# Issuing each pass of a float32r product as two matmuls of 256 columns

## The chip, the cores and the metric

The kernel runs on one core of one Trainium2 chip. The metric is the device time of that core in microseconds. The profile gives the time from the first to the last instruction (the span) of one execution, and the clock granted to TensorE in each stretch (1.00 is 2.4 GHz, 0.5 is 1.2 GHz).

## The reference, cut to what matters

Four residual layers act on 512 tokens of 1024 features, all in float32. Layers 0 and 1 have a mixer and a feed-forward part, each with a modulated norm; blocks 2 and 3 have mixers of several gated branches and a feed-forward part with a short convolution. Nearly all arithmetic is in products of activations with weights, such as

```
def swiglu(h, w_gate, w_up, w_down):
    return (jax.nn.silu(h @ w_gate) * (h @ w_up)) @ w_down

def mixer_ssd_mla(h, positions, w_in, ...):
    z, xbc, dt_raw, q_a, kv_a, k_pe = split_cols(h @ w_in, L0_SIZES)
    ...
    return jnp.concatenate([y_ssd, o_mla], axis=-1) @ w_out
```

with 512 rows in h, 1024 to 5000 columns in the input weights of the mixers and 2816 hidden features in each feed-forward part (two products up, one down). Between them stand state space scans, gated linear attention, causal and sparse attention, convolutions and norms.

## The kernel before, in words

Activations lie by feature: a tile has 128 features on the partitions and the 512 tokens along the free axis. A float32 product is made of three passes of float32r parts. A weight block [128, 128] is split into a high and a low part (whi by ScalarE, L364; wlo by VectorE, L365), and so is each activation tile (tiles named h for the input of a layer, s for others). The function mm3 (L246) issues the three passes whi·xhi, whi·xlo, wlo·xhi into one PSUM bank of 128 x 512 float32; the weights are the stationary operand and the tokens the moving one. In the trace every matmul has its own LDWEIGHTS, under the engine PEld.

The callers of mm3 are these:

- gemm_group (L269): two m-tiles of output in the banks named pg, all k-tiles of one after all of the other, 512 tokens at a time. The weights come from wtiles (L222) in sets of at most 8 blocks, [128, 1024], so a set serves 24 passes.
- gemm_wide (L302): 3 or 4 m-tiles side by side (banks pg and pa) at the start of a product whose input becomes ready tile after tile. Where the input comes by halves of the tokens, the matmuls have 256 columns already.
- gemm_tail (L281): the last m-tiles of a product by halves of the tokens, also in matmuls of 256 columns, with the norm's work (L387, L421, L2264, L2296) between them.

gemm_tok (L334) has the same three passes with the operands exchanged (L349 to L351): the activations are stationary and the weights move, 512 columns in two of its products and 256 in two others. One of the latter (the values of block 2) takes, for two groups of heads out of three, every fourth token as the stationary operand.

The instructions of each engine are put in order beforehand by a scheduler, by the priority that each had when it was traced (`cur_priority`, which counts instructions); an instruction whose operands are not ready yields to the next. Helpers such as `paced` and `later` shift these priorities, so that the products of a layer run between the small instructions of its attention and scans (L824 to L844, L1940 to L1952 and others). The first matmul into a bank has `start=True`, which clears the whole bank.

Of the kernel before, what the change touches and what calls it, by code (L numbers as in the profile page):

```python
# [26 lines left out]
# order of the work: priorities and steps between what runs side by side, slots and tiles of the phases  # L27
# [21 lines left out]
class Core:  # L49
    """Helpers shared by the layers: weight streaming, float32 products in three passes of float32r  # L50
    parts, norms over features. Activations by feature live in slots of 4 KB a partition."""
# [27 lines left out]
    def consts(self, group, t=None, queue=None):  # L79
        """Load a group of constants, not before the instruction of self.mark has been issued."""  # L80
        if t is None:
            t = self.s4([128, self.a[group].shape[1]])
        if self.mark is None:
            (queue or self.nc.scalar).dma_start(t, self.a[group])
        else:
            with self.tc.issue_after(self.mark.ins):
                self.nc.scalar.dma_start(t, self.a[group])
        self.groups[group] = t
# [12 lines left out]
    # ---- memory: tiles of one tag are handed out in the order traced, so streams of work that are to  # L101
    # run side by side have tags of their own
    @contextmanager
    def psum(self, **banks):
        """The banks of the streams a and b, for the phases in the block."""
        with self.tc.tile_pool(name=self.nm("ps"), bufs=1, space=PSUM) as self.xpool:
            self.banks = banks
            yield
# [28 lines left out]
    def s4(self, shape=(128, 2, T), dt=F32, tag="s4"):  # L137
        """A slot of 4 KB a partition of the phase."""
        return self.spool.tile(list(shape), dt, tag=tag, name=self.nm(tag), bufs=self.nslots[tag] if isinstance(self.nslots, dict) else self.nslots)

    def fa(self, dt=F32, tag="s4"):
        """Tiles of features [128, T], two to a slot, taken when first used."""
# [11 lines left out]
    def h4(self, i, dt=F32):  # L154
        """Slot i % 8 (two tiles of features) of the memory of the input of a layer, free for float32, or for
        float32r parts, in place of those before."""
# [6 lines left out]
    def ha(self, slots, dt=F32):  # L163
        """As fa, in slots of the input of a layer."""
# [11 lines left out]
    def parts(self, tag="s4"):  # L176
        """Tiles of features as float32r parts: x(k) = (high, low). Tag h: the input of a layer."""
# [8 lines left out]
    @contextmanager  # L186
    def later(self, by):
        """What the block traces yields to what is traced up to `by` instructions after it."""
        at = self.tc.cur_priority
        self.tc.cur_priority = at + by  # L190
        yield
        self.tc.cur_priority = at

    @contextmanager
    def paced(self, by):
        """Products traced in the block, and what belongs to them, run between what is traced after it: a step
        of 3 passes every `by` instructions."""
# [10 lines left out]
    def beside(self):  # L208
        """What the block traces has the priority of what is traced after it."""
# [4 lines left out]
    def step(self, at):  # L214
        """The priority of one step of paced products, counted from at."""
# [6 lines left out]
    def wtiles(self, src, blocks):  # L222
        """At most 8 blocks [128, 128] of weights, as float32r parts [128, 1024]."""
# [12 lines left out]
    def wload(self, w, m0, nm, k0, nk):  # L236
        """m-tiles m0.. and k-tiles k0.. of a packed weight [m, 128, k, 128], as float32r parts: nm times a
        function of k."""
# [7 lines left out]
    def mm3(self, ps, w, x, first, last):  # L246
        (wh, wl), (xh, xl) = w, x
        mm = lambda *a, **k: self.nc.tensor.matmul(*a, **k, skip_group_check=True)  # L248
        i = mm(ps, wh, xh, start=first, stop=False)
        mm(ps, wh, xl, start=False, stop=False)  # L250
        self.mm_mark = mm(ps, wl, xh, start=False, stop=last)
        return i

    def gemm(self, w, x, evac, m0=0, nm=None, wide=False, tail=0):
        """For each m-tile of packed w: evac(m, PSUM [128, T]) of w^T x; x(k) gives float32r parts, to be
        scaled by token after the product if there is x.rows. Wide: 4 m-tiles at first, for tiles of x that
        become ready one after the other, or 3 by halves of the tokens where x does. Tail: the last m-tiles
        by halves of the tokens, with evac(m, PSUM of the half, its slice)."""
# [22 lines left out]
    def gemm_tail(self, w, x, evac, m0, n):  # L281
        """At most 24 blocks of weights, loaded once. What follows the first half runs under the second."""
# [19 lines left out]
    def gemm_wide(self, w, x, evac, m0, n):  # L302
# [5 lines left out]
        for half in halves:  # L308
            for k in range(nk):
# [3 lines left out]
                for m in range(n):  # L313
                    # the first product of a bank clears it for both halves
# [19 lines left out]
    def gemm_tok(self, w, x, evac, n0=0, n=None):  # L334
        """By token: evac(j, PSUM [128, n]) of x^T w for the 4 tiles of tokens; w packed [128, k, N], n <= 512."""
# [5 lines left out]
        for k0 in range(0, nk, kc):  # L341
            kk = min(kc, nk - k0)
            hi, lo = (t.rearrange("p (k n) -> p k n", n=n) for t in self.wtiles(w[:, k0 : k0 + kk, n0 : n0 + n], kk * n // 128))
            for q in range(kk):
                k = k0 + q
                wh, wl = hi[:, q], lo[:, q]
                for j in range(4):
                    xh, xl = x(k, j)
                    nc.tensor.matmul(pss[j][:, :n], xh, wh, start=k == 0, stop=False)  # L349
                    nc.tensor.matmul(pss[j][:, :n], xl, wh, start=False, stop=False)  # L350
                    nc.tensor.matmul(pss[j][:, :n], xh, wl, start=False, stop=k == nk - 1)  # L351
# [8 lines left out]
    def split(self, hi, lo, src, scale=None):  # L360
        """hi + lo = src (times a per-partition scale), both float32r."""
# [10 lines left out]
    def sq_acc(self, acc, src, first, scale=1.0):  # L372
        """acc (+)= (src scale) squared."""
# [8 lines left out]
    def tok_sums(self, tiles, p=None, first=True, last=True):  # L382
        """[128, 4] by token in PSUM: sums over the partitions of all tiles. Not first: added to a bank with sums."""
# [6 lines left out]
    def pow_rstd(self, p, n, eps, pool=False):  # L390
        """(p / n + eps) ** -0.5 for a few columns p."""
# [8 lines left out]
        # Newton's method, from half the exponent: 3.5e-2, 2e-3, 5e-6, rounding  # L400
# [7 lines left out]
    def rstd_tok(self, tiles, n, eps=EPS, pool=False):  # L408
        """[128, 4] by token: (sum over partitions and tiles / n + eps) ** -0.5."""
        return self.pow_rstd(self.tok_sums(tiles), n, eps, pool)  # L410

    def bcast_tok(self, r):
        """[128, 4] by token -> PSUM [128, T], the same on every partition."""
# [4 lines left out]
    def bcast_to(self, p, r, j0):  # L418
        """[128, n] by token, of the tiles j0.. of tokens, into p."""
# [19 lines left out]
    def norm_h(self, r, x, gain, shift=None, update=None, h=None, half=slice(0, T)):  # L439
        """float32r parts of x rows gain (+ shift), by feature; r [128, T] the rows. update(k) completes x(k).  # L440
        With h: the half of the tokens of h."""
# [20 lines left out]
    def set_rows(self, h):  # L462
        """At the start of a phase: the factors by token that its input lacks, on all partitions."""
# [5 lines left out]
    def ffn(self, h, up, down, conv, end):  # L469
        """down^T (silu(gate) * val), with gate and val through a causal convolution of 3 where conv gives  # L470
        its taps; end() gives the evac of the product and what follows it."""
# [29 lines left out]
def _cols(w, idx):  # L501
    """Columns of w by index, zeros where it is -1, packed as [m, 128, k, 128]."""
# [13 lines left out]
def _tok(w):  # L516
    """[K, N] as [128, K / 128, N]."""
# [3 lines left out]
def _pv(a):  # L521
    """A vector by feature as [128, n]."""
# [9 lines left out]
def _taps(w):  # L532
    """[taps, channels] -> [128, channels / 128 * taps]."""
# [8 lines left out]
# l0_w_in: z 0, xbc 1024, dt 2560, q_a 2576, kv_a 2960, k_pe 3216  # L542
# [5 lines left out]
# l1_w_in: gq 0, gk 512, gv 1024, glr 2048, gg 2064, nq 3088, kc vc ks vs kw vw 3600 + 128 i, ngate 4368  # L548
# [26 lines left out]
# w_in_2: q 0, k 768, v 1536, conf_a 2304, conf_gate 3072, sc_b 3840, sc_c 4608, sc_x 5376, gates 6144 + 1024 b  # L575
# [23 lines left out]
# w_in_3: r k v 512 i, wl 1536, al 1600, gl 1664, qkv 1792, z 3328, a 3840, b 3844, gate_a 3848, gate_b 4872  # L599
# [90 lines left out]
def _lvl(s, u):  # L690
    """For each level of halves of 2 ** l tokens: s in the first and t in the second half of one block."""
# [6 lines left out]
def _lvls(f, n, levels, odd):  # L698
    """For each level f(p, 128 level + u), at the columns u < n in the first (odd: second) halves of blocks."""
# [29 lines left out]
def _dist2(p, u, dil, span):  # L729
    """p + span - u steps back, of dil tokens each; 1e30 outside 0 .. 128 steps."""  # L730
# [40 lines left out]
class Layer0:  # L771
    """SSD and latent attention, with the input and output projections."""
# [21 lines left out]
    def conv_evac(self, out, ps, w, taps, bias=None):  # L794
        """out[t] = bias + sum_s w(taps - 1 - s) ps[t - s]: a causal convolution along the free axis."""
# [8 lines left out]
    def silu_half(self, out, u):  # L804
        """out = silu(2 u)."""
# [5 lines left out]
    def softplus(self, out, x, shape):  # L811
        """out = max(x, 0) + ln(1 + exp(-|x|))."""
# [7 lines left out]
    def attn_scores(self, q, k, w, bias, l, m=None):  # L820
        """exp(s - max s) of s = q^T k + bias for one block of 128 queries, and its sums l."""
# [9 lines left out]
    def attn_pv(self, o, p, w, v, even=True):  # L831
        """o [128 queries, dv] += p v, with v(kb) the values of key block kb."""
# [13 lines left out]
    def pipeline(self, units, steps=1):  # L846
        """Run generators with each step of a unit traced next to the step before of the unit after it. Steps: those
        after the first of the last unit."""
# [124 lines left out]
    def attn_out(self, out, ot, blk):  # L973
        """[128 tokens, 512 features] into 4 tiles by feature."""
# [8 lines left out]
    def l0_ssd(self, xbc, zs, misc, cs, fill):  # L983
        """silu(z) (y + d x) of the state space scan into the tiles of x, by chunks of 128 tokens and 4 heads
        at a time."""
        nc = self.nc
        # steps, decays
# [96 lines left out]
class Layer1:  # L1084
    """Gated linear attention and native sparse attention. The selection holds every block of keys
    (there are no more blocks than it selects) and the window every key, so both are causal attention
    over all keys, whatever the compressed scores."""
# [1444 lines left out]
```

## Time and profile before

| what | value |
|---|---|
| three timed runs, us | 3772.47, 3777.20, 3788.69; median 3777.2 |
| profiled execution, span, us | 3789.9 (no other time is given for it) |
| busy share of the span | PE 97%, PEld 78%, DVE 58%, ACT 36%, POOL 6% |
| matmuls, loads of weights | 20496, 20496 |
| mean granted TensorE clock | 0.979 |
| DMA | 99 GB/s over the span |

PE is the matmul unit and PEld its weight load, which runs beside it. DVE is VectorE, ACT is ScalarE, POOL is GpSimd. A record of a matmul lasts from its start to the end of its results, so that in a dense stream the records overlap: the time that one takes of the engine is the distance from its start to the start of the next, which is read from a timeline or from the count in a window, not from the mean duration of a record.

### The profile page before, as it was taken

The page shows a single profiled execution, that of the slowest core. Times are in us where ns is not written, and L with a number is a line of the kernel's source. Part 1 is how long each engine was busy: PE and PEld are TensorE (multiplying, and loading weights), DVE is VectorE, ACT ScalarE, POOL GpSimd, SP SyncE. Part 2 cuts the span into 40 slices and gives each one's busy share as a digit, 9 for nine tenths or more (in the row PEclk, how much of TensorE's full clock was granted, in tenths as well). Part 3 has the DMA queues.
Part 4 walks back from the last instruction along what each step waited for, and adds up shares of the span by engine and source line. Part 5 has one row for each costly group of instructions (what it writes and reads, how often), then busy time and mean ns, then how long its engine had stood idle before and what let it go on. Part 6 is the DMA issues. An engine that isn't in the chain of part 4 may idle for free.

```text
span 3789.9 us, 50851 instructions
## 1 busy us (share of the span) xinstructions
PE 3690.6 (97%) x20496; PEld 2946.1 (78%) x20496; DVE 2194.6 (58%) x3803; ACT 1357.0 (36%) x2197; POOL 242.3 (6%) x214
## 2 busy tenths in 40 slices
PE   7998999999999999999999999999999999999999
PEld 5776788877887778877878888788877777887887
DVE  7866655454377653338629354665466656766652
ACT  5344432324254432322332243443343332334432
POOL 2003100110022100101000010000000000100000
PEclk9998999999999999999989999999999999999999
DMA  6511265533310242333112234223321121152232
GB/s 217 181 47 56 99 201 188 167 111 98 119 31 23 66 152 94 117 95 103 57 39 73 84 102 138 90 95 116 93 98 40 61 69 43 32 178 89 95 117 73
DMA packets 120219, 373.75 MB, mean 99 GB/s; under 512 B 12064, under 2 KB 20128, under 8 KB 119984
## 3 DMA queue, kind: packets, MB, share of 16 engines
q1 hardware_dynamic: 105008, 322.05, 26.0%
q10 hardware_dynamic: 14976, 48.45, 3.8%
q8 instruction: 161, 2.64, 0.3%
q14 instruction: 74, 0.61, 0.1%
HBM read 349.49 MB, written 20.97 MB: 98 GB/s over the span
## 4 chain that ended last, share of the span: by engine, by line
PE 91%; DVE 6%; ACT 1%; issue 1%; DMA 0%; POOL 0%; POOLq 0%; DVEq 0%; ACTq 0%
PE pg L248 68%; PE pa L248 3%; PE pb L844 2%; PE pb L824 1%; PE pb L837 1%; PE pb L1264 1%; DVE wlo L365 1%; PE pa L387 1%; PE pg L1351 1%; PE pb L2264 1%; DVE wa L2142 1%; PE pg L349 0%; PE pa L349 0%; PE pa L350 0%; PE pg L350 0%
## 5 line engine op out<-in xcount | busy, mean ns | idle before, releaser
L248 PE MATMUL pg<-h,whi 128*128 128x512 f32 (+1 forms) x5584 | 1801.3, 401 | 44.8 <-ACT h L458 14.9
L248 PEld LDWEIGHTS pg<-h,whi 128*128 128x128 f32 x5584 | 1047.1, 190 | 307.3 <-ACT h L458 18.7
L248 PE MATMUL pg<-h,wlo 128*128 128x512 f32 (+1 forms) x2792 | 1113.4, 399 | 0.0
L364 ACT ACTIVATE whi<-wraw 128x1024 fp32r<-128x1024 f32 (+3 forms) x540 | 547.0, 1014 | 1414.7 <-PE pg L248 1106.1
L365 DVE TENSOR_TENSOR wlo<-wraw,whi 128x1024 fp32r<-128x1024 f32 (+3 forms) x540 | 639.2, 1185 | 665.2 <-ACT whi L364 662.4
L248 PE MATMUL pg<-s,whi 128*128 128x512 f32 (+1 forms) x2044 | 629.7, 390 | 2.6 <-DVE s L906 2.4
L248 PEld LDWEIGHTS pg<-h,wlo 128*128 128x128 f32 x2792 | 532.3, 191 | 123.5 <-issue 3.7
L248 PEld LDWEIGHTS pg<-s,whi 128*128 128x128 f32 x2044 | 379.1, 189 | 94.5 <-DVE s L906 3.7
L248 PE MATMUL pg<-s,wlo 128*128 128x512 f32 (+1 forms) x1022 | 397.3, 389 | 0.0
L248 PEld LDWEIGHTS pg<-s,wlo 128*128 128x128 f32 x1022 | 192.5, 188 | 43.5
L802 DVE SCALAR_TENSOR_TENSOR td<-td,vec,td 128x511 f32<-128x511 f32 (+1 forms) x188 | 139.9, 747 | 59.5 <-ACT td L798 57.9
L2142 DVE CUSTOM_DVE_ANT_0 wa<-wa,scb,vec 128x1024 f32<-128x1024 f32 x90 | 121.7, 1354 | 71.3 <-DMA wa<-in_l_ada_dram 71.2
L327 DVE TENSOR_TENSOR td<-pg,rows 128x512 f32<-128x512 f32 x130 | 89.7, 691 | 98.3 <-PE pg L248 98.0
L1500 DVE SCALAR_TENSOR_TENSOR s<-s,vec,s 128x504 f32<-128x504 f32 (+25 forms) x180 | 121.4, 731 | 0.4
L844 PEld LDWEIGHTS pb<-s,tb 128*128 128x128 f32 x600 | 83.6, 198 | 31.3 <-DVE tb L842 9.3
L248 PE MATMUL pa<-h,whi 128*128 128x512 f32 (+1 forms) x336 | 97.1, 363 | 0.0
L364 ACT ACTIVATE s<-td 128x512 fp32r<-128x512 f32 x94 | 59.3, 630 | 102.3 <-DVE td L489 102.0
L844 PE MATMUL pb<-s,tb 128*128 128x64 f32 x600 | 90.7, 281 | 2.9 <-DVE tb L842 2.9
L365 DVE TENSOR_TENSOR s<-td,s 128x512 fp32r<-128x512 f32 x94 | 66.9, 712 | 31.1 <-ACT s L364 31.1
L489 DVE TENSOR_TENSOR td<-td,pg 128x512 f32<-128x512 f32 x44 | 30.3, 688 | 80.9 <-PE pg L248 80.9
L248 PEld LDWEIGHTS pa<-h,whi 128*128 128x128 f32 x336 | 61.2, 194 | 10.1
L798 ACT ACTIVATE td<-td,vec 128x512 f32<-128x512 f32 x94 | 66.4, 708 | 4.5 <-DVE td L327 3.1
(804 smaller groups left out, 4140.4 us busy)
## 6 DMA issues: line engine op xcount, KB each, us to landing
wraw<-in_b_in_dram SPq DMA_DIRECT2D x112, 512.0 KB, 3.2
wraw<-in_l_up_dram SPq DMA_DIRECT2D x88, 512.0 KB, 3.2
wraw<-in_b_up_dram SPq DMA_DIRECT2D x88, 512.0 KB, 3.2
wa<-in_l_ada_dram ACTq DMA_DIRECT2D x80, 512.0 KB, 3.3
wraw<-in_l_in_dram SPq DMA_DIRECT2D x51, 512.0 KB, 3.3
wraw<-in_l_down_dram SPq DMA_DIRECT2D x32, 512.0 KB, 3.5
wraw<-in_b_down_dram SPq DMA_DIRECT2D x32, 512.0 KB, 3.5
xd<-s SPq DMA_DIRECT2D x28, 512.0 KB, 2.7
```

What stands on the lines that cost most here:

```text
L248: mm = lambda *a, **k: self.nc.tensor.matmul(*a, **k, skip_group_check=True)
L327: self.nc.vector.tensor_mul(y, ps, rows)
L364: i = nc.scalar.activation(hi, src, AF.Copy)
L365: nc.vector.tensor_sub(lo, src, hi.bitcast(F32))
L387: self.pe_mark = self.nc.tensor.matmul(p[:, j : j + 1], t[:, j * 128 : j * 128 + 128], self.c("ones"), start=first and i + j == 0, stop=la ...
L798: nc.scalar.activation(out, ps, AF.Copy, scale=w(taps - 1))
L802: nc.vector.scalar_tensor_tensor(out[:, s:], ps[:, : T - s], w(taps - 1 - s), out[:, s:], ALU.mult, ALU.add)
L824: nc.tensor.matmul(s[:, :w], q, k, start=True, stop=True)
L837: nc.tensor.transpose(pt[:, b * 128 : b * 128 + 128], p[:, b * 128 : b * 128 + 128], self.ident)
L844: nc.tensor.matmul(o, st[:, b * 128 : b * 128 + 128], v(b), start=b == 0, stop=b == nb - 1)
L1500: nc.vector.scalar_tensor_tensor(out[:, s:], x[:, : T - s], tap(30 - s), out[:, s:], ALU.mult, ALU.add)
L2142: nc.vector.tensor_tensor_reduce(w, w, self.scb, 1.0, b, ALU.mult, ALU.add, o)
```

## The change

mm3 issues each of its three passes in pieces of at most 256 columns. For a bank of 512 columns these are two matmuls with the same stationary operand, one for the first half of the bank and one for the second. Only the first piece of the first pass clears the bank, and the second piece of that pass is held behind it. All pieces of a pass are traced with the same priority, so that the count of priorities is as before. gemm_tok calls mm3 in place of three matmuls of its own. Matmuls that had 256 columns stay as they were. The diff also takes out comments and docstrings, which are left out here.

```diff
     def mm3(self, ps, w, x, first, last):
         (wh, wl), (xh, xl) = w, x
-        mm = lambda *a, **k: self.nc.tensor.matmul(*a, **k, skip_group_check=True)
-        i = mm(ps, wh, xh, start=first, stop=False)
-        mm(ps, wh, xl, start=False, stop=False)
-        self.mm_mark = mm(ps, wl, xh, start=False, stop=last)
-        return i
+        n = ps.shape[-1]
+        cols = [slice(c, min(c + T // 2, n)) for c in range(0, n, T // 2)]
+        out = None
+        for a, b, head, tail in ((wh, xh, first, False), (wh, xl, False, False), (wl, xh, False, last)):
+            at = self.tc.cur_priority
+            for c in cols:
+                self.tc.cur_priority = at
+                with self.tc.issue_after(out.ins) if head and out else nullcontext():
+                    i = self.nc.tensor.matmul(ps[:, c], a, b[:, c], start=head and c.start == 0, stop=tail, skip_group_check=True)
+                out = out or i
+        self.mm_mark = i
+        return out
...
     def gemm_tok(self, w, x, evac, n0=0, n=None):
...
                 for j in range(4):
-                    xh, xl = x(k, j)
-                    nc.tensor.matmul(pss[j][:, :n], xh, wh, start=k == 0, stop=False)
-                    nc.tensor.matmul(pss[j][:, :n], xl, wh, start=False, stop=False)
-                    nc.tensor.matmul(pss[j][:, :n], xh, wl, start=False, stop=k == nk - 1)
+                    self.mm3(pss[j][:, :n], x(k, j), (wh, wl), k == 0, k == nk - 1)
                     at = self.step(at)
```

## Rows read from the trace of the kernel before

**Rows 1.** Page, head and part 1: span, and busy us of each engine.
```profile
span 3789.9 us, 50851 instructions
PE 3690.6 (97%) x20496; PEld 2946.1 (78%) x20496; DVE 2194.6 (58%) x3803; ACT 1357.0 (36%) x2197; POOL 242.3 (6%) x214
```
**Rows 2.** Page, part 4: the chain that ended last, by engine and by line.
```profile
PE 91%; DVE 6%; ACT 1%; issue 1%; DMA 0%; POOL 0%; POOLq 0%; DVEq 0%; ACTq 0%
PE pg L248 68%; PE pa L248 3%; PE pb L844 2%; PE pb L824 1%; PE pb L837 1%; PE pb L1264 1%; DVE wlo L365 1%; PE pa L387 1%; PE pg L1351 1%; PE pb L2264 1%; DVE wa L2142 1%; PE pg L349 0%; PE pa L349 0%; PE pa L350 0%; PE pg L350 0%
```
**Rows 3.** Windows: busy us (count of records) of each engine, clock, DMA.
```profile
472.00:792.00 320.00, 320.00 (x1373) 257.81 (x1373) 173.36 (x220) 97.62 (x126) 10.86 (x7) 1.00 0.55 178
1346.00:1666.00 320.00, 320.00 (x1373) 257.84 (x1372) 120.99 (x139) 96.64 (x126) 10.84 (x7) 1.00 0.35 113
2398.50:2730.50 332.00, 332.00 (x1425) 267.49 (x1424) 193.63 (x244) 127.04 (x166) 0.00 (x0) 1.00 0.31 99
3445.00:3760.00 315.00, 315.00 (x1352) 252.45 (x1351) 180.53 (x225) 115.76 (x148) 0.00 (x0) 1.00 0.30 96
```
**Rows 4.** The whole span, L248 alone: PE busy (count), PEld busy (count).
```profile
0.00:3789.90 3789.90, 2915.16 (x12210) 2249.27 (x12210) 0.98 0.30 99
```
**Rows 5.** Groups by line, operation and shape; count, then busy us, mean ns.
```profile
L248 PE MATMUL pg<-h,whi 128*128 128x512 f32 x5392 | 1763.3, 405 | 38.4 <-ACT h L458 11.7 <-DVE h L459 8.9 <-DVE td L327 5.9
...
L349 PE MATMUL pa<-whi,h 128*128 128x512 f32 x32 | 12.7, 395 | 0.0
...
L248 PE MATMUL pg<-sb,wlo 128*128 128x512 f32 x32 | 12.5, 390 | 0.0
...
L349 PE MATMUL pg<-whi,s 128*128 128x512 f32 x4 | 1.6, 398 | 0.0
```
**Rows 6.** Windows as in rows 3, in runs of matmuls of 256 columns.
```profile
424.10:432.90 8.80, 8.80 (x80) 8.80 (x79) 4.88 (x9) 2.62 (x7) 0.00 (x0) 1.00 0.18 61
895.30:904.90 9.60, 9.60 (x87) 9.60 (x86) 2.90 (x4) 1.06 (x1) 0.00 (x0) 1.00 0.33 109
1297.30:1306.00 8.70, 8.70 (x79) 8.70 (x79) 4.80 (x9) 2.53 (x7) 0.00 (x0) 1.00 0.19 60
3774.10:3779.20 5.10, 5.10 (x47) 5.10 (x46) 2.71 (x8) 0.00 (x0) 0.00 (x0) 1.00 0.60 207
1808.50:1818.00 9.50, 9.50 (x83) 9.50 (x82) 9.41 (x16) 1.77 (x4) 0.00 (x0) 1.00 0.38 110
3766.80:3771.40 4.60, 4.60 (x41) 4.60 (x41) 0.42 (x1) 0.20 (x1) 0.00 (x0) 1.00 0.02 4
466.30:469.80 3.50, 3.50 (x32) 3.50 (x32) 2.51 (x7) 0.78 (x2) 0.00 (x0) 1.00 0.78 236
1339.50:1343.00 3.50, 3.50 (x32) 3.50 (x31) 2.48 (x7) 0.81 (x2) 0.00 (x0) 1.00 0.79 231
```
**Rows 7.** Timeline of PEld at 3766 us: start, us, and the count merged.
```profile
3765.65 0.97 PEld L387 LDWEIGHTS pb<-cst,td 128*128 128x128 f32 x8
3766.55 0.30 PEld L248 LDWEIGHTS pg<-s,whi 128*128 128x128 f32 x2
```
**Rows 8.** Timeline of PE: first passes after other work, 512 and 256 columns.
```profile
1831.17 0.50 PE L248 MATMUL pg<-h,whi 128*128 128x512 f32 x1
1831.51 0.40 PE L248 MATMUL pg<-h,wlo 128*128 128x512 f32 x1
...
3766.57 0.48 PE L248 MATMUL pg<-s,whi 128*128 128x256 f32 x2
3766.89 0.28 PE L248 MATMUL pg<-s,wlo 128*128 128x256 f32 x1
```
**Rows 9.** Window as in rows 3, in small matmuls of 64 x 64 and less.
```profile
3276.80:3295.20 18.40, 18.40 (x391) 14.46 (x386) 11.15 (x18) 5.64 (x10) 0.00 (x0) 1.00 0.06 17
```
**Rows 10.** Timeline at 1946 us: 256 columns, every fourth token stationary, and its loads.
```profile
1946.03 0.40 PE L351 MATMUL pa<-wlo,h 128*128 128x256 f32 x1
1946.26 0.40 PE L349 MATMUL pg<-whi,h 128*128 128x256 f32 x1
...
1946.13 0.33 PEld L349 LDWEIGHTS pg<-whi,h 128*128 128x128 f32 x1
1946.36 0.33 PEld L350 LDWEIGHTS pg<-whi,h 128*128 128x128 f32 x1
```

## The prediction

> **What bounds the kernel now.** I read the page's engine shares first, then the chain of waits, then windows of the long products, then the groups by shape, and last the runs in which the matmuls already have 256 columns. The shares show TensorE busy in 3690.6 of 3789.9 us [rows 1], and the chain that ended last is 91% TensorE, 68% of it the passes of L248 into the banks pg [rows 2]. But overlapping records are busy whatever their rhythm, so neither says what one pass costs. The windows of the four feed-forward parts do. In them nothing but L248 runs on TensorE, the clock is at 2.4 GHz, and VectorE has work for 173.36 of 320.00 us at the most in the first, ScalarE for 97.62 [rows 3]. A window counts every record that touches it, so the rhythm is (length + one record) / count: (320.00 + 0.39) / 1373 = 233.3 ns from start to start, and the other three windows give the same to 0.1 ns. So the bound is the rate at which TensorE takes passes of 512 columns, and the change touches just that.
>
> **How many.** L248 has 12,210 matmuls, each with a load of its own, though the first two passes of mm3 use the same whi [rows 4]: a repeated operand is loaded again. By shape, ten groups of L248 with 512 columns (from x5392 to x32, first and last in [rows 5]) add up to 11,502; the other 708 have 256 and stay. The six groups of L349 to L351 of x32 and the six of x4 (one of each kind in [rows 5]) add 216. Together 11,718 passes become 23,436 matmuls with as many loads.
>
> **What two halves cost.** The trace already has runs of such matmuls, with the same operands and lines, and there are two rhythms [rows 6]. By the same formula with a record of 0.28 us, the first window gives (8.80 + 0.28) / 80 = 113.5 ns and the fifth (9.50 + 0.28) / 83 = 117.8 ns. The first four windows are of the fast kind (113.5 to 114.5), the last four of the slow (117.8 to 119, the short ones coarser by their edges). Each kind occurs in products by feature and by token, with DMA at 4 to 236 GB/s, with VectorE idle or full; the first and third windows are the same code of two layers, as are the last two. A run keeps its rhythm until something interrupts it. So a pair costs 227.0 ns (6.3 less than one pass of 512) or 235.6 (2.3 more). What picks the rhythm the rows do not show; I take it as drawn anew at each interruption, with the odds seen: 80 + 87 + 79 + 47 = 293 records fast, 83 + 41 + 32 + 32 = 188 slow, 61% fast. Then a matmul costs 0.61 x 113.5 + 0.39 x 117.8 = 115.2 ns, a pair 230.4, which is 2.9 ns under 233.3.
>
> Bounds of this term: all slow, 11,718 x 2.3 ns = +27 us; all fast, 11,718 x 6.3 ns = -74 us. I take the mean, 11,718 x 2.9 = -34 us, since both rhythms were met in rows of this very shape, and keep both ends for the range.
>
> The Trainium skill has a rule against the change: TensorE: Matmul & The Clock Gate, section Back-to-back issue gap, gives a warm matmul N / 2.4 + 2.5 ns, thus 215.8 for 512 columns and 109.2 for 256, with the fixed part paid twice after the change. By that page the estimate is 11,718 x 2.5 = +29 us. The trace doesn't agree for 512 columns, at 233.3 [rows 3]; its slow rhythm has that rule's sign, its fast one doesn't [rows 6].
>
> **What else is added or moved.**
> *Loads.* Eight loads in front of matmuls of one column follow each other at (0.97 - 0.19) / 7 = 111 ns [rows 7], so loads alone could go on at 111 ns and the fast rhythm of 113.5 is just above them: after the change the load unit is nearly full where it had half its time free. That is inside the 113.5 and 117.8, so it is not counted again.
> *Starts.* After foreign work the first pass of 512 columns holds the engine for 1831.51 - 1831.17 = 0.34 us. Two of 256 take 3766.89 - 3766.57 = 0.32 [rows 8]. The difference of some -0.02 us, or of the opposite sign at another start, I cost at nothing: even 400 starts of 0.02 us are 8 us either way, which the range holds.
> *Instructions.* 23,436 more instructions (11,718 matmuls and loads) pass TensorE's queue. In the small matmuls 391 records go by in 18.40 us, 47 ns for a load and a matmul [rows 9], against some 115 needed, so issuing them costs nothing; if it did bind, it would be at the 47 ns and not at 115.
> *Order and waits.* No wait, DMA or instruction of another engine is added. SP's, ACT's and POOL's queues are untouched. The pieces share one priority, so on TensorE the stream keeps its order against the small work; a shift by a few instructions where the scheduler finds operands ready earlier is possible, and I cost it at nothing, bounded by the 99.3 us that TensorE is now idle in the whole span (3789.9 - 3690.6 [rows 1]), of which a part could come or go.
> *Cover.* What TensorE gains must not be lost to the next engine. A set of weights serves 24 passes, 5.6 us; VectorE is idle for 146.6 of 320 us in the tightest long window and ScalarE for 222 [rows 3], so 24 x 2.9 = 70 ns less per set leaves the splits hidden. In the mixers VectorE is on the chain for 6% of the span [rows 2]; if no pass outside the four long windows gained anything, 1373 + 1373 + 1425 + 1352 = 5,523 passes would remain and the gain would be 16 us.
>
> **Sum.** 3789.9 - 34 = 3755.9 us of span. The profiled execution lies 12.7 us above the median of the timed runs, 0.3%, too little to scale a term of 34 us, so the forecast is 3777.2 - 34 = 3743 us.
>
> **Rivals.**
> *All fast.* If the fast rhythm is the one that long undisturbed streams settle in, all passes gain 6.3 ns: 3777.2 - 74 = 3703. For it: three of the four longest windows of rows 6 are fast. Against it: the fourth, at 1808.50, holds the slow rhythm for 83 matmuls.
> *All slow, slower than before.* Each matmul pays a fixed part on top of its columns, and two pay it twice: from 2 x 117.8 - 233.3 = 2.3 ns a pass, 3777.2 + 27 = 3804. For it: the 512-column stream keeps one rhythm through all four long windows, so the 256-column one may also do so, and the two windows right before feed-forward streams (466.30 and 1339.50) are slow. Against it: 61% of the records. It decides as soon as the fast share falls under 2.3 / (2.3 + 6.3) = 27%.
> *No change.* The fast share lands near 27%, or the gain of the mixers is lost to VectorE and the long streams gain little: within 0.5%, about what a measurement here can tell from no change, 3758 to 3796; I put it at 3777.
> *The load becomes the bound.* With every fourth token stationary a load lasts 0.33 us, and the matmuls of 256 columns stand 1946.26 - 1946.03 = 0.23 us apart [rows 10], as far as those of 512. At that price for each half the change would add 11,718 x 0.23 = 2.7 ms. Against it: the operands of the changed passes are contiguous, as those of rows 6 are.
> *It doesn't do what it says.* If the second load of the same operand were dropped, the stream would have fewer loads and be at or under the fast case. Against it: 12,210 loads for 12,210 matmuls [rows 4].
>
> **How the numbers follow.** Forecast (mixture, 3723 to 3758) 0.45; all fast 0.20; no change 0.16; all slow 0.15; load bound 0.02; dropped loads 0.02. Faster by over 0.5%: 0.45 + 0.20 + 0.02 = 0.67; within 0.5%: 0.16; slower: 0.15 + 0.02 = 0.17. The range takes in the all-fast case and the all-slow one with 2 to 3 us beside each, for the small terms: 3700 to 3806. The forecast's own range is 3723 to 3758.
>
> **What would show it.** In the profile after: 32,214 matmuls and as many loads (20,496 + 11,718); mean distance in the four feed-forward windows of 113.5 or 117.8 ns, each kept for a long stretch, and not one value between; busy time of PEld up to nearly that of PE; DVE and ACT unchanged in busy time. It is wrong if the distance is something else, such as over 119, if one rhythm holds everywhere, if the number of loads is not doubled, or if TensorE's idle time grows by more than 10 us.

## The result, and the profile after

The change made the kernel slower: 3817.11 us (median of five runs, 3814.17 to 3847.32) against 3781.89 for the kernel before on the same chip, a ratio of 1.0106 (95% interval 1.0069 to 1.0142). A second measurement gave 1.0121 (1.0088 to 1.0155). The forecast was 3743 us, and the range ended at 3806, so the change went the other way and past the range.

The profiled execution of the kernel after is its slowest run, 3847.32 us, so a second profile of it (span 3797.0 us) stands beside it below. The page, with the span, part 1 and the chain, answers to [rows 1, 2]:

```profile
span 3845.1 us, 74316 instructions
PE 3723.8 (97%) x32214; PEld 3536.5 (92%) x32214; DVE 2192.9 (57%) x3803; ACT 1357.8 (35%) x2197; POOL 242.4 (6%) x214
...
PE 86%; DVE 7%; DMA 3%; issue 2%; ACT 1%; POOL 1%; POOLq 0%; DVEq 0%; ACTq 0%
```

The counts are as foreseen: 32,214 matmuls and as many loads, DVE and ACT unchanged. But TensorE's idle time is 3845.1 - 3723.8 = 121.3 us, where it was 99.3 [rows 1], and the chain has 86% of TensorE where it had 91%. The mean clock is 0.965, where it was 0.979.

Windows of the kernel after inside the feed-forward streams of layer 1, block 2 and block 3, and in a stretch of block 3's mixer (columns as in rows 3):

```profile
1400.00:1680.00 280.00, 280.00 (x2380) 280.00 (x2379) 100.26 (x112) 83.58 (x109) 10.84 (x7) 1.00 0.34 106
2480.00:2760.00 280.00, 280.00 (x2473) 280.00 (x2472) 169.33 (x214) 112.53 (x147) 0.00 (x0) 1.00 0.33 103
3520.00:3800.00 280.00, 280.00 (x2473) 280.00 (x2472) 167.07 (x211) 106.62 (x137) 0.00 (x0) 1.00 0.34 104
3400.00:3460.00 60.00, 60.00 (x499) 59.70 (x498) 39.24 (x54) 24.89 (x34) 0.00 (x0) 1.00 0.63 205
```

By the formula of the prediction the first is (280.00 + 0.28) / 2380 = 117.8 ns a matmul and the next two 113.3: the two rhythms of [rows 6], each kept for 280 us. So the long streams did what was foreseen, two of them 18 us faster together (2,777 passes by 6.6 ns). The loss must lie elsewhere. To find it I aligned both traces by the 540 splits of weights (the starts of ScalarE's whi), which come in the same order, and compared the time between them. Two places stand out, which lose 53 us together.

The mixer of layer 1, between the same two splits, before and then after (windows, columns as in rows 3):

```profile
1063.60:1246.50 182.90, 176.07 (x1229) 141.26 (x1228) 139.91 (x438) 91.62 (x242) 46.18 (x53) 0.99 0.05 16
```
```profile
1068.90:1282.60 213.70, 197.58 (x1262) 158.81 (x1261) 146.23 (x444) 92.63 (x243) 50.15 (x55) 0.90 0.04 13
```

That is +30.8 us for the same work, with a few more records for the cut passes: TensorE is idle 16.1 us in place of 6.8, and busy 21.5 us longer at a mean clock of 0.90 in place of 0.99 (42.8 us of it at 1.2 GHz, 4.1 before). In the second profile the stretch takes 206.3 us.

The norm in the mixer of block 2, where 48 matmuls of one column sum a mean. First all of them before (operation, count, durations in ns, first and last start in us), then after:

```profile
L387 PE MATMUL pa<-cst,s x48: 164/250/250, 2002.2 to 2126.6; 128*128 128x1 f32 x48
```
```profile
L394 PE MATMUL pa<-cst,s x48: 164/250/352, 2262.8 to 2268.6; 128*128 128x1 f32 x48
```

Before, they ran as their tiles became ready, in groups over 124 us, and VectorE made the mean from them at 2127.6 us, 16 us before TensorE first used it. After, they stand in one block just ahead of that use (2269.0 and 2270.2 us). What follows shows in the timeline of TensorE after (start, length, count, and the idle time before with what ended it) and in its waits there:

```profile
2262.76 6.17 PE L394 MATMUL pa<-cst,s 128*128 128x1 f32 x48
2270.22 1.91 PE L428 MATMUL pa<-cst,rsa 128*128 128x128 f32 x8
2283.51 1.02 PE L394 MATMUL pa<-cst,ta 128*128 128x1 f32 x8 [0.45 <-DVE ta L387]
2287.90 2.04 PE L428 MATMUL pa<-cst,rya 128*128 128x128 f32 x8 [3.02 <-DVE rya L412]
```
```profile
PE pg L259 <- ACT s L371: 5.3, 1, 5.3
PE pa L428 <- DVE rya L412: 3.0, 1, 3.0
```

The whole norm now lies on the path: 8.7 us of waits, and 20.5 us at 1.2 GHz where there were none. Between the same splits this part took 67.0 us and takes 89.6 (91.0 in the second profile); before, then after:

```profile
2187.80:2254.80 67.00, 67.00 (x297) 54.03 (x296) 39.84 (x62) 31.36 (x49) 7.78 (x4) 1.00 0.30 94
```
```profile
2218.20:2307.80 89.60, 80.69 (x637) 79.44 (x637) 39.35 (x63) 32.20 (x49) 7.00 (x4) 0.89 0.23 72
```

The order of the two built programs says the same. Of TensorE's 16,930 passes and small matmuls 4,307 stand more than 3 places from where they stood, 263 of them more than 60, nearly all in the four mixers; in the long streams none has moved by more than 3. The other engines are not as before either: of VectorE's instructions 840, of ScalarE's 238 stand more than 3 places off in the trace. So theory A: the cut changed the order that the scheduler makes, and the order costs the time. Its rivals: B, twice the matmuls and loads pull the clock down; C, a fixed part per matmul, paid twice.

### The profile page after: what moved, and what is told of

Same layout as the page of the kernel before. It is cut to its first block, busy times and chain, and to the rows that moved or that the text cites. A ratio compares the mean times of both kernels' runs of the same rounds, so it can differ in the third digit from the quotient of the medians.

```text
span 3845.1 us, 74316 instructions
## 1 busy us (share of the span) xinstructions
PE 3723.8 (97%) x32214; PEld 3536.5 (92%) x32214; DVE 2192.9 (57%) x3803; ACT 1357.8 (35%) x2197; POOL 242.4 (6%) x214
## 4 chain that ended last, share of the span: by engine, by line
PE 86%; DVE 7%; DMA 3%; issue 2%; ACT 1%; POOL 1%; POOLq 0%; DVEq 0%; ACTq 0%
PE pg L259 65%; PE pa L259 4%; DMA wa<-in_l_ada_dram 2%; PE pb L851 2%; PE pb L831 1%; PE pb L844 1%; PE pb L1271 1%; DVE wa L2149 1%; DVE wlo L372 1%; PE pa L1065 1%; PE pb L2271 1%; PE pa L428 1%; PE pg L1358 1%; PE pa L394 1%; ACT whi L371 0%
## 5 line engine op out<-in xcount | busy, mean ns | idle before, releaser
L259 PE MATMUL pg<-h,whi 128*128 128x256 f32 x10976 | 1813.5, 285 | 48.7 <-ACT h L465 18.4
L259 PEld LDWEIGHTS pg<-h,whi 128*128 128x128 f32 x10976 | 1514.6, 192 | 79.8 <-ACT h L465 21.0
L259 PE MATMUL pg<-h,wlo 128*128 128x256 f32 x5488 | 1124.6, 284 | 0.0
L259 PEld LDWEIGHTS pg<-h,wlo 128*128 128x128 f32 x5488 | 859.1, 192 | 7.0 <-issue 3.2
L259 PE MATMUL pg<-s,whi 128*128 128x256 f32 x3968 | 627.2, 280 | 9.8 <-ACT s L371 5.3
L259 PEld LDWEIGHTS pg<-s,whi 128*128 128x128 f32 x3968 | 534.7, 189 | 16.8 <-ACT s L371 5.6
L259 PE MATMUL pg<-s,wlo 128*128 128x256 f32 x1984 | 396.4, 279 | 0.0
L259 PEld LDWEIGHTS pg<-s,wlo 128*128 128x128 f32 x1984 | 305.0, 189 | 0.0
L1507 DVE SCALAR_TENSOR_TENSOR s<-s,vec,s 128x498 f32<-128x498 f32 (+25 forms) x180 | 121.2, 724 | 0.4
L259 PE MATMUL pa<-h,whi 128*128 128x256 f32 x544 | 96.4, 287 | 0.0
L805 ACT ACTIVATE td<-td,vec 128x512 f32<-128x512 f32 x94 | 66.5, 710 | 10.9 <-DVE td L1454 7.8
```

The lines of the kernel that those rows point to most:

```text
L259: i = self.nc.tensor.matmul(ps[:, c], a, b[:, c], start=head and c.start == 0, stop=tail, skip_group_check=True)
L805: nc.scalar.activation(out, ps, AF.Copy, scale=w(taps - 1))
L1507: nc.vector.scalar_tensor_tensor(out[:, s:], x[:, : T - s], tap(30 - s), out[:, s:], ALU.mult, ALU.add)
```

## The experiments

**Order and cut apart.** `pin` chains the matmuls of a kernel in a given order (a list of numbers); the cut and the order can then be combined at will.

```diff
+def pin(tc, nc, second):            # at the end of the trace
+    ...
+    for k in ORDER:
+        for i in units[k]:           # a pass, with both halves where it is cut
+            if prev is not None:
+                tc.add_manual_dep(i, prev.name, NoSync, reason="pin")
+            prev = i
```

> Halves as in the change, but TensorE's matmuls are chained in the order in which they stood before the change (the two halves of a pass side by side); nothing is left out. Theory A (the changed order of TensorE's work in the mixers costs the time, the halves themselves earn a little): the long streams keep what they show in the profile after, some -2.4 us or +0.8 us per 15 sets of weights, and the layer 1 mixer and the norm of block 2 lose their +25.6 and +22.5 us; 3750 to 3775 us, TensorE idle about 100 us and at 1.2 GHz about 160 us as before. Theory B (twice as many matmuls and loads lower the granted clock by themselves): 3805 us or more, over 220 us at 1.2 GHz. Theory C (a fixed part per matmul, paid twice, in the mixers): 3790 to 3810 at the idle and clock of before.

Measured: 3812.23 us, ratio 1.0082 (1.0054 to 1.011). A miss for theory A as it stood. The norm lost nothing (67.5 us), but the layer 1 mixer took 199.5: with TensorE's order held, ScalarE's and VectorE's had still moved (332 of VectorE's instructions by more than 3 places). By its time alone this run fits theory B. Its profile, of one of its faster executions, does not: it has 135 us at 1.2 GHz, where theory B said over 220. So the run decides little by itself.

> Passes of 512 columns as before the change, but TensorE's matmuls are chained in the order that they have after it; nothing is left out. Theory A: slower than before by the mixers' part of the loss, 3805 to 3840 us, with the same idle time and the same stretch at 1.2 GHz in the layer 1 mixer and in the norm of block 2. Theories B and C: 3770 to 3790 us, as before, since no matmul is cut.

Measured: 3842.69 us, ratio 1.0172 (1.0151 to 1.0192): +63 us with not one matmul cut. The layer 1 mixer took 209.2 us and the norm's part 92.1. Its page and its windows of the two places:

```profile
span 3840.8 us, 50852 instructions
PE 3717.2 (97%) x20496; PEld 2961.3 (77%) x20496; DVE 2194.8 (57%) x3803; ACT 1357.2 (35%) x2197; POOL 241.5 (6%) x214
...
PE 89%; DVE 6%; issue 2%; ACT 2%; POOL 1%; DMA 0%; POOLq 0%; DVEq 0%; ACTq 0%
```
```profile
1067.30:1276.50 209.20, 195.50 (x1228) 154.75 (x1227) 143.82 (x443) 91.44 (x242) 47.24 (x53) 0.91 0.04 14
2204.20:2296.30 92.10, 83.48 (x355) 67.66 (x354) 39.42 (x63) 32.19 (x49) 7.00 (x4) 0.87 0.22 70
```

The idle time is 123.6 us with the matmuls of before. B and C, which said 3770 to 3790, can't explain that. Nor can the DMA that has 3% of the chain in the kernel after, since it has 0% here. `pin` holds TensorE alone here, and the other engines moved with it: 741 of VectorE's instructions and 228 of ScalarE's stand more than 3 places from where they stood before. So the +63 us are the price of TensorE's order together with what it draws after it. What TensorE waits for in this mixer (total us, times, longest), before and with the new order:

```profile
PE pg L1351 <- DVE h L1354: 2.2, 1, 2.2
PE pg L248 <- DVE h L365: 1.8, 2, 1.0
PE pb L844 <- DVE tb L842: 1.0, 3, 0.4
```
```profile
PE pg L1355 <- POOL ta L1345: 4.1, 4, 1.3
PE pb L848 <- DVE tb L846: 3.7, 3, 2.3
PE pg L252 <- DVE h L369: 3.1, 2, 2.3
```

The same code (its line numbers are 4 higher here) now waits 4.1 us for GpSimd, where it waited 0.2 us before, and longer for VectorE: the streams of small work cover each other less.

> The kernel after the change, unchanged, for a second profile. Theory A: the layer 1 mixer (about 214 us between its two sets of weights, 183 before) and the norm of block 2 (22 us more than before) show their loss again, since the order of the instructions is fixed when the program is built; 3810 to 3820 us. If the profile shows neither again at such a time, the first profile's two places were chance, and the loss lies elsewhere.

Measured: 3833.02 us, ratio 1.0121 (1.0088 to 1.0155), with 206.3 us in the layer 1 mixer and 91.0 in the norm's part. The time is above the 3810 to 3820 expected, but both places are there again, at another rhythm of the long streams. So the two places belong to the program and not to one execution.

> Halves in the four feed-forward parts alone, 512 columns elsewhere; nothing is left out. Theory A: no loss of order, since TensorE's order stays as before there, and each part by its rhythm: all fast 5,523 x -6.3 ns = -35 us, all slow +13 us, as in the profile after (two parts fast, two slow) -12 us; 3740 to 3790, likeliest 3765. Theory B: the clock falls also here, 3790 or more. Theory C: +13 us, 3790.

```diff
-        cols = [slice(c, min(c + T // 2, n)) for c in range(0, n, T // 2)]
+        w0 = T // 2 if self.halve else T     # halve: only inside ffn()
+        cols = [slice(c, min(c + w0, n)) for c in range(0, n, w0)]
```

Measured: 3771.23 us, ratio 0.9987 (0.9966 to 1.0008), 12 runs from 3753 to 3791. The time fits theory A and not B or C (3790 us), but the gain is not told from zero. In its profile three of the four streams are fast (windows, as in rows 3), and its span is 3763.3 us, 26.6 under that of the profile before (one execution each):

```profile
490.00:610.00 120.00, 120.00 (x1022) 120.00 (x1021) 69.35 (x93) 33.23 (x44) 0.00 (x0) 1.00 0.64 192
1360.00:1640.00 280.00, 280.00 (x2473) 280.00 (x2472) 105.51 (x119) 86.19 (x112) 10.85 (x7) 1.00 0.37 113
...
3440.00:3720.00 280.00, 280.00 (x2473) 280.00 (x2472) 167.29 (x210) 106.81 (x137) 0.00 (x0) 1.00 0.34 103
```

The two places take 182.8 and 67.0 us here, as before. That also clears the rest of the edit: gemm_tok goes through mm3 here too, by which its second and third pass have changed places, and none of the four stretches with a mixer is more than 1 us longer than before.

**All five engines held.** The same chain, for ScalarE, VectorE, GpSimd and SyncE as well, DMAs included:

> Halves as in the change, but the instructions of all five engines are chained in the order of the kernel before (with TensorE's order alone held, ScalarE's and VectorE's still moved in the mixers, and the layer 1 mixer kept +16.7 of its +23 to +31 us); nothing is left out. Theory A (order alone costs): the layer 1 mixer falls back to 183 us between its two sets of weights, with about 4 us at 1.2 GHz and 7 us idle, the norm of block 2 stays at +0.4, and what is left is the rhythm of the halves: 3725 to 3770 us. Theory B (more matmuls and loads pull the clock down in the mixers): layer 1 keeps +10 us or more and about 30 us at 1.2 GHz, 3790 to 3815 us.

Measured: 3775.42 us, ratio 0.9982 (0.9965 to 1.0). The page and the window of the layer 1 mixer:

```profile
span 3777.9 us, 74309 instructions
PE 3678.2 (97%) x32214; PEld 3510.7 (93%) x32214; DVE 2194.3 (58%) x3803; ACT 1357.3 (36%) x2197; POOL 242.0 (6%) x214
```
```profile
1071.10:1255.30 184.20, 177.37 (x1254) 144.52 (x1252) 140.37 (x438) 91.54 (x242) 46.00 (x53) 0.98 0.05 15
```

All 32,214 matmuls and loads are there, and the loss is gone: 99.7 us idle, 184.2 us in the mixer (6.8 of them idle, 7.1 at 1.2 GHz), 66.5 in the norm's part, a mean clock of 0.977 to 0.985 over its runs, where those of before have 0.973 to 0.985. The time is 5 us above the range of theory A and well under that of theory B, which falls.

> The kernel with the halves and the order of before on all five engines, once more, to narrow the interval of its first measurement (0.9982, 0.9965 to 1.0) and for a second profile. If the halves by themselves earn what their mean rhythm in five profiles gives (115.6 to 116.4 ns a half where 116.65 would be even: 0.5 to 2 ns a pass, 6 to 24 us over 11,718 passes, less the passes that stand alone): 3760 to 3775 us. If they earn nothing: 3775 to 3785.

Measured: 3768.87 us, ratio 0.9947 (0.9927 to 0.9966), again with 99.7 us idle (3771.9 - 3672.2). The two measurements of one kernel do not quite agree: by their ratios the cut alone earns 7 us (0 to 13) in the first and 20 us (13 to 28) in the second. It is the only version that a measurement puts clear of the kernel before, by about half a per cent.

> Halves everywhere but in the four feed-forward parts, each engine's order as the scheduler makes it (TensorE's is that of the kernel after but for some hundred places); nothing is left out. Theory A: all of the loss of order and only a part of the gain, 3820 to 3860 us, with the layer 1 mixer at +20 to +30 us and the norm of block 2 at +24, and a scatter between runs narrower than that of the kernel after, since the four long streams have one rhythm again. Theory C (fixed part per matmul): the loss follows the share of the cut passes, half of them here, 3795 us.

The edit is the flag of the feed-forward run with its two values exchanged. Measured: 3838.6 us, ratio 1.0142 (1.011 to 1.0174), four runs within 19 us, 214.1 us in the layer 1 mixer and 89.0 in the norm's part. Theory C, with 3795, falls too.

**The order, mixer by mixer.** Each takes one stretch of the new order into the kernel before:

```diff
-    ORDER = order of before
+    ORDER = before[:u] + after[u:v] + before[v:]   # u, v: where one mixer begins and ends
```

> Passes of 512 columns and TensorE's order of before, but in the layer 1 mixer (649 of the 16,930 passes and small matmuls) its order of after; nothing is left out. If each mixer's own order sets its loss: +20 to +26 us, 3800 to 3806, with 200 to 210 us between the mixer's two sets of weights (183 before) and some 40 us at 1.2 GHz there. If the loss needs what comes before it (another start, another rhythm): within 5 us of before.

Measured: 3805.33 us, ratio 1.0078 (1.0057 to 1.0099), against 3778.06: +27 us, with 201.8 us in the mixer, 26.9 of them at 1.2 GHz.

> The same with the order of after in the mixer of block 2 alone (1,683 places), where the 48 matmuls of one column that sum the mean of the norm stand in one block before their use and not 90 us and more ahead of it. If each mixer's own order sets its loss: +20 to +26 us, 3800 to 3806, the wait in the norm (8 us idle, 20 us at 1.2 GHz) as in the profile after. If not: within 5 us of before.

Measured: 3794.71 us, ratio 1.0051 (1.0035 to 1.0067): +17 us, a little less than expected, with the norm's part at 88.6 us and the layer 1 mixer at 182.9. There the chain holds the order of before, and the mixer takes what it took without a chain, so the chain itself costs nothing there.

> The same with the order of after in the mixer of block 3 alone (3,627 places). If the three mixers add up to the +63 us of all of the new order: +8 to +18 us, 3787 to 3797. If the loss is in the two other mixers alone: within 5 us of before.

Measured: 3798.74 us, ratio 1.0055 (1.0037 to 1.0073): +21 us, a little more than expected. Which waits make it was not traced. The three add up to +65 us, and the whole new order costs +63: each mixer pays for its own order, whatever runs before it. The mixer of layer 0, where 301 places moved by more than 3, was not run alone; the sum leaves nothing for it, and the stretch with it takes 456 us with the whole new order, 455 before (one execution each).

> The kernel after the change, TensorE's order in the mixer of block 2 alone put back to that of before; nothing is left out. If order is the cause: the norm's +24 us go and the rest of the loss stays, 3792 to 3805 (its own runs spread over 40 us). If not: 3815 to 3835 as the kernel after.

Measured: 3803.48 us, ratio 1.0048 (1.0023 to 1.0074), where the kernel after has 1.0106 and 1.0121; the norm's part is back at 67.3 us and the layer 1 mixer still takes 203.7. One part undone gives its part back.

## Why the prediction was wrong

The step that failed is "Order and waits": "on TensorE the stream keeps its order against the small work; a shift by a few instructions [...] is possible, and I cost it at nothing, bounded by the 99.3 us that TensorE is now idle". The pieces do share one priority, and in the long streams, from whose windows I argued, nothing moved. But in the mixers nearly all of the 4,307 places that moved by more than 3 lie, and VectorE's and ScalarE's order moved with them; the prediction called ScalarE's queue untouched. With the matmuls uncut that order costs +63 us (+27, +17 and +21 by mixer). What made the scheduler choose otherwise I did not trace: that it chose otherwise after the cut is shown, the reason stays open.

The bound was no bound either. Idle time that is there says nothing about idle time to come: it grew from 99.3 us to 121 with the change and to 124 with the new order alone. And there is a second price that the prediction has nowhere, the clock. Windows of the layer 1 mixer after (as in rows 3):

```profile
1090.00:1100.00 10.00, 8.08 (x35) 6.65 (x35) 5.15 (x22) 2.79 (x14) 2.46 (x2) 0.65 0.16 52
1100.00:1110.00 10.00, 10.00 (x64) 9.57 (x63) 3.76 (x13) 2.99 (x8) 0.00 (x0) 0.67 0.01 2
1110.00:1120.00 10.00, 7.60 (x53) 5.47 (x53) 9.03 (x36) 5.25 (x15) 4.42 (x6) 1.00 0.00 1
1120.00:1130.00 10.00, 10.00 (x37) 7.27 (x37) 6.09 (x21) 3.62 (x12) 2.96 (x4) 0.52 0.01 2
1130.00:1140.00 10.00, 10.00 (x36) 7.71 (x37) 6.74 (x21) 3.15 (x8) 3.09 (x5) 0.50 0.00 1
...
1150.00:1160.00 10.00, 9.71 (x74) 8.01 (x72) 8.52 (x28) 3.07 (x9) 0.00 (x0) 1.00 0.01 2
```

TensorE waits 2.29 us just before 1091.8 us, and 1.20 us each before 1113.2 and 1118.3. The granted clock is at 1.2 GHz from 1093.0 to 1106.7 and from 1120.3 to 1140.8 us, and at 2.4 GHz between and after (0.65 and 0.67 are means over both levels). What that costs shows in the same group of eight matmuls at 1.2 and at 2.4 GHz (start, length):

```profile
1122.25 1.97 PE L851 MATMUL pb<-s,tb 128*128 128x64 f32 x8
1145.62 1.00 PE L851 MATMUL pb<-s,tb 128*128 128x64 f32 x8
```

In the two places together, the kernel with the new order uncut is 15.5 us longer idle than the kernel before (13.7 and 8.6 us against 6.8 and 0.0) and 57.9 us longer at 1.2 GHz (38.1 and 23.9 us against 4.1 and 0.0). If all that runs there goes at half the speed, the latter costs 29 us, an estimate; with the idle time that makes about 44 of the 51 us which the two places lose. That the waits bring the lower clock is read from what comes first, and from both coming together in every profile with the new order of a place; no run changes one without the other. Elsewhere the clock falls without them: in the stretch between the feed-forward parts of layer 1 and block 2, three uncut kernels that keep TensorE's order there, with 7 us idle each, are at 1.2 GHz for 51, 17 and 92 us (the kernel before and those with the new order in block 3 or layer 1 alone).

The other steps:

- *What two halves cost.* Right in kind, too high in size. The rhythms of 113.3 and 117.8 ns came as read from [rows 6], each in long stretches. Counted in groups of 24 matmuls in a row without a gap, at 2.4 GHz, the fast share was 41 to 64% in six profiles with all passes cut (61% forecast), the mean 115.0 to 116.0 ns (115.2 forecast, 116.65 is even). Where the share came out near 61% that is in part luck: each long stream mostly keeps one rhythm, so a profile has few draws. The term of -34 us measured -7 and -20 us with the order held. One row was missing: in the stretch of block 3's mixer in the window at 3400 us, a half takes (60.00 + 0.28) / 499 = 120.8 ns. There 512 columns had a rhythm of their own before, (30.00 + 0.39) / 134 = 226.8 ns:

```profile
3370.00:3400.00 30.00, 30.00 (x134) 24.86 (x133) 18.84 (x26) 13.26 (x19) 0.00 (x0) 1.00 0.63 208
```

  so that a pair loses 14.8 ns and not 2.3. I had taken 233.3 for every pass, and a distance over 119 was on my list of what would prove the forecast wrong.
- *Loads, instructions.* Right: no load was dropped, PEld is busy 92%, and neither loads nor issue set a rhythm outside those of [rows 6], but for the 120.8.
- *Starts.* Not told apart by any run.
- *Cover.* Right in three long streams, though the tightest of them by VectorE was misread: it is the third window of [rows 3], with 193.63 of 332 us, and not the first, with 173.36 of 320. In the stream of layer 0 TensorE waits for VectorE, 3.6 us in the first profile and 3.4 in the second, which it did not before; with every engine's order held that wait is absent too.
- *The rule of the Trainium skill.* The estimate of +29 us by that rule (TensorE: Matmul & The Clock Gate, section Back-to-back issue gap) lies near the loss, but the runs don't bear it out: with the order held, twice the matmuls cost less time, not more. The section itself calls that formula the gap of an isolated matmul and says that it misses the spacing of a stream, so it was no rule for these streams.
- *Rivals.* "All slow", 3804 us, came nearest in time and was wrong in its reason: about half of the long streams ran fast. None of my rivals had the order as its mechanism, though one sign of it, idle time up by more than 10 us, was on my list of what would prove the forecast wrong, and that is what came.

## What to carry to other kernels

Where a scheduler orders the instructions, an edit that only cuts instructions is two edits, and the second is a new order: compare the orders of the two programs before pricing the first, above all in the stretches with small work. Hold the old order by a chain and measure again; here the cut alone earned 7 to 20 us and the new order cost 63. Price a new wait on TensorE with the clock around it, not by its own length alone: in two mixers here 15.5 us more idle time came with 57.9 us more at 1.2 GHz. And compare stretches between the same instructions, not whole spans: the two profiles of the kernel after spend 271 and 159 us at 1.2 GHz, and their spans differ by 48 us.

## What the runs showed of the hardware

The rhythm of matmuls of 256 columns can change at an interruption. In the second profile of the kernel after, layer 0's stream runs at (80.00 + 0.28) / 681 = 117.9 ns, stops for about 1 us at 570 us, waiting for VectorE, and goes on at (50.00 + 0.28) / 443 = 113.5 with the same operands (windows, as in rows 3):

```profile
480.00:560.00 80.00, 80.00 (x681) 80.00 (x680) 44.48 (x62) 21.67 (x29) 0.00 (x0) 1.00 0.59 187
580.00:630.00 50.00, 50.00 (x443) 50.00 (x443) 29.42 (x40) 14.74 (x19) 0.00 (x0) 1.00 0.60 197
```

The first profile of the same kernel keeps 117.8 ns in this stream until a stop of 3.6 us at 658 us and goes on at 113.3; with every engine's order held there is no stop, and the stream keeps 117.8 ns to its end. In all seven profiles in which it is cut, the stream of layer 0 starts at 117.8 ns, so the rhythm is not simply drawn by lot.

In other streams the same program can be fast in one execution and slow in the next: layer 1's ran at 117.8 ns in the first profile of the kernel after (x2380 in 280 us, above) and at 113.3 in the second, block 2's the other way round (x2473, then x2379):

```profile
1370.00:1650.00 280.00, 280.00 (x2473) 280.00 (x2472) 108.24 (x122) 87.14 (x114) 10.84 (x7) 1.00 0.36 116
2430.00:2710.00 280.00, 280.00 (x2379) 280.00 (x2379) 165.18 (x208) 107.54 (x139) 0.00 (x0) 1.00 0.32 100
```

5,523 passes of the long streams by 8.6 ns between the rhythms are 47 us. The runs of the kernels with all passes cut spread over 28 to 60 us each, those of the kernel before over 19 to 33; how much of that the rhythm makes and how much the clock is not shown. What picks the rhythm stays open.
